# A hybrid encoder step on one core: norm weights beside x's rows, two weight loads on ScalarE's queue, and a newly recorded order

## The chip, the core and the metric

The kernel runs on one core of one Trainium2 chip. The metric is the device time of one execution in microseconds (us), as the median of several. The kernel before takes 340.26 us, the median of three runs (340.23 to 340.39).

## What is computed

One layer of a streaming encoder for 512 prompt tokens (with 256 memory tokens) and for 32 new tokens over caches of 512 to 1024 rows, all in float32:

```
z = rmsnorm(x, norm_mix_g) @ w_in            # 1024 -> 3880 columns: q, k, v and gate of A and B, q and gate of M, indexer
mk, mv = rmsnorm(mem, norm_mem_g) @ w_mem_kv
oa = attention over the own and the 8 earlier chunks, with a learned position bias   # 6 heads x 64
ob = attention over the keys that an indexer picks (top 128 of prompt, 256 of 1056)  # 6 heads x 64, rotary
om = attention over the 256 memory tokens                                            # 4 heads x 64
x  = x + concat(oa * silu(ga), ob * silu(gb), om * silu(gm)) @ w_out
y  = rmsnorm(x, norm_final_g)                # and the new k and v rows are outputs too
```

## The kernel before

**Split products.** Each large product is done as three matmuls in a rounded format: a factor v is rounded on ScalarE to `h` (`xTh`, `wh`, `oAh`), and `l = v - h` (`xTl`, `wl`, `oAl`) is made on VectorE or GpSimd; the product is `h*h + l*h + h*l`. x comes in turned: eight blocks of 128 columns of x, `xr`, each 128 partitions by 544 tokens (512 prompt, 32 sample). The norm weight of a row of `xr` is a scalar of its partition, so that `A.activation(..., scale=gT[0][:, k:k+1])` scales and rounds in one pass. `gT[0]` (`g_mix` in the trace) is a tile of its own, loaded by a small DMA.

**The order is recorded, not scheduled by a tool.** The helper class `Timed` (all instructions stand under line 411) hands each instruction to the engine's program at once and also to `Line`, a small planner inside the kernel that keeps a clock for each engine. Tasks are Python generators that yield the time at which they want to go on; `Line.run` issues TensorE's projections one after the other and lets waiting tasks slip in between. So numbers such as `HOLD`, `LAG` and `SURE`, the costs in `Line.cost` and `Line.rate`, and the lists `START` (first loads), `EARLY` and `LATE` (order of the projections) decide the order in which instructions stand on every engine, and nothing else.

**TensorE.** Most of its work uses the array as 128x128. Attention scores (`k,q`) use it as two tiles of 64 rows, attention outputs (`z,va`, `z,vb`) as two of 64 columns, and the products of the 32 sample tokens (`raw,xF`, `xr,gw`, `raw,oS`) as four of 32 columns. `divided` issues such a job: it waits up to `HOLD` us (in the planner's clock) for another such job and then issues them together. `places` counts the score tiles that may be live (`SCORES`).

**The start.** `x_load` loads x block by block, and for each block 296 columns of the indexer's weights (`raw`); `ahead_load` adds 128 columns of the first key projection `ka0`. All go out on SyncE's queue (SP). `index_group` multiplies the two as they come; before data is there, TensorE multiplies a tile of ones.

**Who makes `wl`.** `w_split` gives a subtraction to VectorE when GpSimd is 0.5 us behind VectorE in the planner's clock, else to GpSimd. The rotary embedding (`rope_t`) shuffles and multiplies on VectorE (`rq`, `kb`, `qb`); the last addition goes to the less loaded of the two. `picks` is the top-128 search (`ysel`, `m`) on VectorE; `sample_choice` finds the threshold for the 32 sample tokens.

Of the kernel before, what the change touches and what calls it, by code (L numbers as in the profile page):

```python
# [36 lines left out]
START = "xxxwwwwtrrrrrwmmrr"  # L37
SURE = 1.0
SLACK = 1.06
HOLD = 2.0  # L40
LAG = 0.3
# [52 lines left out]
class Line:  # L94
# [4 lines left out]
    def __init__(self):  # L99
        self.clk = {"PE": 1.35, "DVE": 0.7, "ACT": 0.9, "POOL": 1.2, "SP": 0.7}  # L100
# [60 lines left out]
    @staticmethod  # L161
    def lag(of, to):

        if of is None and to == "PE":
            return 0.3
        if of == to or of is None:
            return 0.127 if to == "DVE" else 0.09 if to == "POOL" else 0.0
        return 0.95 if of == "SP" else 0.26 if to == "PE" else 0.2 if of == "PE" else 0.06 if of == "POOL" else 0.15
# [69 lines left out]
    def rate(self):  # L238

        t = self.clk["SP"]  # L240
        return 340e3 if t < 1 else 170e3 if t < 2.3 else 330e3 if t < 7 else 310e3 if 11 < t < 22 else 370e3

    def op(self, eng, op, outs, ins, kw):
# [16 lines left out]
        d = (outs[0].size() * 4 / self.rate() if eng == "SP" else  # L260
# [33 lines left out]
    def begin(self, o, t):  # L294
        last = self.last
        o.start = t
        if o.eng == "SP":
            o.end = max(t + 1.3, last["DMA"]) + o.d
            o.after = {"SP": t + 0.45, "DMA": o.end}
# [12 lines left out]
        self.clk[o.eng] = o.end if o.eng != "SP" else t  # L312
# [127 lines left out]
def hybrid_step(ctx: ExitStack, tc: tile.TileContext, a: dict):  # L440
# [3 lines left out]
    V, G, A, PE, DMA = (Timed(line, n, e) for n, e in (("DVE", nc.vector), ("POOL", nc.gpsimd), ("ACT", nc.scalar),  # L444
                                                       ("PE", nc.tensor), ("SP", nc.sync)))
# [44 lines left out]
    def divided(k, issue):  # L490
# [3 lines left out]
        job = [k, issue, None, False]  # L494
        waiting.append(job)
        end = line.now() + HOLD
        while not job[3]:
            if len(waiting) == 1 and line.now() < end:
# [5 lines left out]
            for j in [job] + [j for j in waiting if j is not job]:  # L504
                if there(j[0]):
# [136 lines left out]

    def w_split():
        for i in range(len(w_list)):
# [26 lines left out]
            if i < 4:  # L671
                for kk in range(2):
                    yield line.at(raw[:, kk, :])
                    rounded(wh[:, kk, :], raw[:, kk, :])
                    yield line.at(wh[:, kk, :]) - 0.2
# [7 lines left out]
            tsub(V if i in WV or 0.5 < line.clk["POOL"] - line.clk["DVE"] else G, wl, raw, f(wh))  # L683
# [124 lines left out]
    gT = [cp.tile([P, NK], F32, name=n) for n in ("g_mix", "g_mem")]  # L808
# [1480 lines left out]
```

## Time and profile before

| | |
|---|---|
| median of the timed runs | 340.26 us |
| the profiled execution: own time / span in the trace | 340.1 us / 338.3 us |
| TensorE (PE) busy | 329.9 us, 98%, 2785 matmul records |
| VectorE (DVE), ScalarE (ACT), GpSimd (POOL) busy | 283.2, 219.9, 166.1 us |
| granted TensorE clock | 9 of ten or more in every fortieth of the span |
| HBM read / written | 39.95 / 6.16 MB |

The span is what the trace covers; the profiled execution's own time is 1.8 us longer. A matmul's duration in the trace overlaps its successor's, so what a matmul costs is read from start to start. PEld is the weight load that runs ahead of each matmul.

### The profile page before, as it was taken

Reading aid. Unit: us, or ns where it says so; the run is one execution under the profiler, and the core shown is the slowest. Engines: PE = TensorE matmul, PEld = TensorE weight load, DVE = VectorE, ACT = ScalarE, POOL = GpSimd, SP = SyncE. Lnnn points to the kernel's source line nnn. Section 1 sums busy time; section 2 is a strip of 40 time slices with the busy share of each in tenths; the row PEclk is TensorE's granted clock in tenths of the full one; section 3 lists DMA queues with packets and bytes.
Section 4 is the critical chain, followed back from the end, with each engine's and each line's share of the span. In section 5 each row is a group of like instructions: output and inputs, shape, how many; then the busy total and the mean of one; then the engine's idle time right before and its main releaser. Section 6 shows DMA issues by size and latency. Waiting matters only on the chain.

```text
span 338.3 us, 7679 instructions
## 1 busy us (share of the span) xinstructions
PE 329.9 (98%) x2785; PEld 296.4 (88%) x2785; DVE 283.2 (84%) x726; ACT 219.9 (65%) x523; POOL 166.1 (49%) x191
## 2 busy tenths in 40 slices
PE   8999999999999999999999999999999999999992
PEld 8979997999998989998999999899998776878682
DVE  3957878698989999699999999999979899865762
ACT  5838787898758786776776755532469446864362
POOL 2326261585453389246257764685338513361542
PEclk9999999999999999999999999999999999999999
DMA  7999763176539412314113343141332977002033
GB/s 219 382 302 344 202 219 105 33 216 160 157 84 304 143 58 58 94 37 136 49 33 74 103 140 97 48 117 42 98 127 65 334 296 273 0 2 95 0 114 152
DMA packets 44725, 46.61 MB, mean 138 GB/s; under 512 B 4400, under 2 KB 36720, under 8 KB 44688
## 3 DMA queue, kind: packets, MB, share of 16 engines
q1 hardware_dynamic: 44688, 46.13, 44.0%
q8 instruction: 22, 0.36, 0.4%
q14 instruction: 15, 0.12, 0.1%
HBM read 39.95 MB, written 6.16 MB: 136 GB/s over the span
## 4 chain that ended last, share of the span: by engine, by line
PE 80%; DVE 9%; issue 4%; POOL 3%; ACT 2%; DMA 1%; POOLq 0%; DVEq 0%; ACTq 0%
PE bank L411 80%; DVE gate L411 1%; DVE ysel L411 1%; DVE m L411 1%; DVE xr L411 1%; DMA raw<-in_w_mem_kv_dram 1%; DVE z L411 1%; DVE KSs L411 1%; POOL wl L411 1%; DVE rot L411 1%; POOL wI L411 1%; POOL rot L411 1%; DVE bi L411 0%; ACT junk L411 0%; POOL rs L411 0%
## 5 line engine op out<-in xcount | busy, mean ns | idle before, releaser
L411 POOL TENSOR_TENSOR wl<-raw,wh 128x512 fp32r<-128x512 f32 (+1 forms) x65 | 90.7, 1398 | 107.3 <-ACT wh L411 105.5
L411 PE MATMUL bank<-xTh,wh 128*128 128x272 f32 x352 | 77.0, 299 | 0.1
L411 ACT ACTIVATE wh<-raw 128x512 fp32r<-128x512 f32 (+3 forms) x85 | 52.0, 619 | 37.2 <-PE bank L411 11.8
L411 PE MATMUL bank<-xTh,wl 128*128 128x272 f32 x352 | 73.0, 288 | 0.0
L411 PE MATMUL bank<-xTl,wh 128*128 128x272 f32 x352 | 72.8, 288 | 0.0
L411 PEld LDWEIGHTS bank<-xTh,wh 128*128 128x128 f32 x352 | 55.6, 189 | 5.2 <-issue 4.1
L411 ACT ACTIVATE z<-z,st 128x128 f32<-128x128 f32 (+3 forms) x78 | 41.0, 549 | 22.9 <-DVE st L411 22.9
L411 PEld LDWEIGHTS bank<-xTh,wl 128*128 128x128 f32 x352 | 55.2, 189 | 0.6 <-issue 0.6
L411 PEld LDWEIGHTS bank<-xTl,wh 128*128 128x128 f32 x352 | 55.2, 188 | 0.5 <-issue 0.5
L411 PE MATMUL bank<-wh,xTh 128*128 128x384 f32 (+1 forms) x88 | 26.9, 336 | 0.0
L411 DVE MAX8 m<-ysel 128x8 f32<-128x256 f32 (+2 forms) x48 | 26.4, 550 | 0.1
L411 PE MATMUL bank<-wh,xTl 128*128 128x384 f32 (+1 forms) x88 | 26.2, 327 | 0.0
L411 PE MATMUL bank<-wl,xTh 128*128 128x384 f32 (+1 forms) x88 | 26.1, 326 | 0.0
L411 DVE MATCH_REPLACE8 ysel<-m,ysel 128x256 f32<-128x256 f32 (+2 forms) x48 | 26.0, 542 | 0.0
L411 DVE SCALAR_TENSOR_TENSOR ysel<-r,wI,ysel 128x256 f32<-128x256 f32 (+2 forms) x21 | 18.6, 885 | 4.2 <-ACT r L411 3.6
L411 ACT ACTIVATE junkS<-ysS,bi 128x1056 int8<-128x1056 f32 x16 | 18.7, 1168 | 4.2 <-DVE bi L411 4.1
L411 PE MATMUL bank<-ident,z 128*128 128x128 f32 (+1 forms) x162 | 21.2, 272 | 0.0
L411 PEld LDWEIGHTS bank<-ident,z 128*128 128x128 f32 (+1 forms) x162 | 17.8, 141 | 2.0 <-issue 0.7
L411 ACT COPY z<-bank 128x512 f32<-128x512 f32 (+2 forms) x31 | 15.2, 517 | 5.5 <-PE bank L411 3.9
L411 ACT ACTIVATE r<-bank 128x512 f32<-128x512 f32 (+3 forms) x30 | 14.0, 485 | 5.8 <-PE bank L411 5.0
L411 PEld LDWEIGHTS bank<-wh,xTh 128*128 128x128 f32 x88 | 15.8, 191 | 0.4 <-issue 0.4
L411 PEld LDWEIGHTS bank<-wl,xTh 128*128 128x128 f32 x88 | 15.7, 188 | 0.0
(286 smaller groups left out, 765.1 us busy)
## 6 DMA issues: line engine op xcount, KB each, us to landing
raw<-in_w_in_dram SPq DMA_DIRECT2D x42, 256.0 KB, 2.9
raw<-in_w_out_dram SPq DMA_DIRECT2D x16, 256.0 KB, 4.1
raw<-in_w_in_dram SPq DMA_DIRECT2D x8, 384.0 KB, 4.0
xr<-in_x_t_dram SPq DMA_DIRECT2D x8, 272.0 KB, 4.3
nat<-in_x_prompt_dram SPq DMA_DIRECT2D x4, 512.0 KB, 5.4
raw<-in_w_mem_kv_dram SPq DMA_DIRECT2D x8, 256.0 KB, 3.1
xr<-in_x_prompt_dram SPq DMA_DIRECT2D x4, 512.0 KB, 6.3
out_dram<-xr SPq DMA_DIRECT2D x4, 512.0 KB, 2.6
```

The source lines that it names most:

```text
L411: return fn(*args, **kw)
```

## The change

`x_t`, the turned x in HBM, gets the norm weights as a 545th column, so that each block of x brings its own; the DMA of `g_mix` goes. The first two weight loads (`DMA2`) are issued on ScalarE's queue. The first block's second half is rounded after the first weights, and the first two blocks are rounded in halves. The planner learns the second queue and other rates, `HOLD`, `LAG` and `SCORES` change, `EARLY` and `LATE` are reordered, `divided` takes a condition, and some subtractions, multiplications and additions are given to GpSimd outright.

```diff
-START = "xxxwwwwtrrrrrwmmrr"
+START = "xxxtwwwwrrrrrwmmrr"
...
-HOLD = 2.0
-LAG = 0.3
+LINK = False
+HOLD = 3.0
+LAG = 0.5
...
-EARLY = ("va", "ka1", "ka2", "mk", "mv", "qa0", "qa1", "ga0", "qa2", "ga1", "ga2", "qm0", "gm0", "qm1", "gm1")
+EARLY = ("va", "qa0", "ka1", "mk", "qa1", "mv", "ga0", "ka2", "qa2", "ga1", "ga2", "qm0", "gm0", "qm1", "gm1")
 AHEAD = "ka0"
-LATE = ("gb0", "kb0", "kb1", "qb0", "qb1", "kb2", "qb2", "vb", "gb1", "gb2")
+LATE = ("gb0", "kb1", "qb0", "kb0", "gb1", "qb1", "vb", "qb2", "gb2", "kb2")
...
-        return 340e3 if t < 1 else 170e3 if t < 2.3 else 330e3 if t < 7 else 310e3 if 11 < t < 22 else 370e3
+        return 340e3 if t < 1 else 250e3 if t < 2.3 else 345e3 if t < 7 else 310e3 if 11 < t < 22 else 370e3
...
-        return When(lambda: max(self.had(x) for x in tiles), SURE + (0.0 if self.now() < 40 else 0.0))
+        return When(lambda: max(self.had(x) for x in tiles), SURE + (0.5 if self.now() < 40 else 0.0))
...
-    def divided(k, issue):
+    def divided(k, issue, may=lambda: True):
...
-            if len(waiting) == 1 and line.now() < end:
+            if not may():
+                yield line.soon()
+                continue
+            if sum(j[4]() for j in waiting) == 1 and line.now() < end and not (LINK and any(j[0] and not j[4]() for j in waiting)):
...
-            tsub(V if i in WV or 0.5 < line.clk["POOL"] - line.clk["DVE"] else G, wl, raw, f(wh))
+            tsub(V if i in WV or 5.0 < line.clk["POOL"] - line.clk["DVE"] else G, wl, raw, f(wh))
...
-        DMA.dma_start(raw, w_in[k0 * P:k1 * P, c0:c0 + P].rearrange("(k p) n -> p k n", p=P))
+        (DMA if ahead else DMA2).dma_start(raw, w_in[k0 * P:k1 * P, c0:c0 + P].rearrange("(k p) n -> p k n", p=P))
...
-            tsub(V if c else V, wl, raw, f(wh))
+            tsub(G if c else V, wl, raw, f(wh))
...
-                DMA.dma_start(gT[0], a["norm_mix_g"])
-            DMA.dma_start(raw[:, kk, :], w_in[rows, QI:QI + 296])
+            (DMA if c + kk else DMA2).dma_start(raw[:, kk, :], w_in[rows, QI:QI + 296])
...
-                if k < 1:
+                if k < 2:
                     for j in range(2):
                         sl = slice(j * N // 2, (j + 1) * N // 2)
-                        yield line.at(t[:, kk, :])
-                        A.activation(h[:, sl], t[:, kk, sl], AF.Copy, scale=gT[0][:, k:k + 1])
+                        if k == 0 and j:
+                            yield from line.wait(lambda: w_k[0] or wh_0)
+                        yield line.at(x)
+                        A.activation(h[:, sl], x[:, sl], AF.Copy, scale=g)
...
-            V.tensor_tensor(t, t, ctab["sin64"][:, sl], op=ALU.mult)
+            G.tensor_tensor(t, t, ctab["sin64"][:, sl], op=ALU.mult)
             yield line.at(t, out) - 0.2
-            least(out, V, G).tensor_tensor(out, t, out, op=ALU.add)
+            G.tensor_tensor(out, t, out, op=ALU.add)
...
-        yield from line.wait(lambda: count["scored"] >= len(TILES) and "kb2" in over)
+        yield from line.wait(lambda: count["scored"] >= len(TILES) and "picks" in over)
...
-    SCORES = 9
+    SCORES = 8
...
-        pair = Pair(0, hp, lambda hp=hp: both(split_q(queried[0][:, hp, 0:S], 1.0, G), split_of(natural["ka"][:, hp, 0:S], 1.0, V, "k")), lambda: va)
+        pair = Pair(0, hp, lambda hp=hp: both(split_q(queried[0][:, hp, 0:S], 1.0, G), split_of(natural["ka"][:, hp, 0:S], 1.0, G, "k")), lambda: va)
...
-    arrays["x_t"] = np.ascontiguousarray(np.concatenate([arrays["x_prompt"], arrays["x_sample"]]).T)
+    g = np.asarray(inputs["norm_mix_g"]).reshape(1, D)
+    arrays["x_t"] = np.ascontiguousarray(np.concatenate([arrays["x_prompt"], arrays["x_sample"], g]).T)
```

What this does to the order of instructions, at three places. First the start of ScalarE's program, before; `xTh` is the rounded x, `wh` a rounded weight (296 columns of the indexer's, 128 or 384 of `ka0`'s):

```order
L411 ACT_TABLE_LOAD
L411 ACTIVATE m_73<-nhalf 128x1
L411 ACTIVATE xTh_79<-xr,g_mix 128x272 x2
L411 ACTIVATE wh<-raw 128x296
L411 ACTIVATE wh<-raw 128x128
L411 ACTIVATE wh<-raw 128x296
L411 ACTIVATE xTh_79<-xr,g_mix 128x544
L411 ACTIVATE wh<-raw 128x384
```

And with the change:

```order
L412 DMA raw<-in_w_in_dram 128x296
L412 DMA raw<-in_w_in_dram 128x128
L412 ACT_TABLE_LOAD
L412 ACTIVATE m_73<-nhalf 128x1
L412 ACTIVATE xTh_79<-xr 128x272
L412 ACTIVATE wh<-raw 128x296
L412 ACTIVATE xTh_79<-xr 128x272
L412 ACTIVATE wh<-raw 128x128
L412 ACTIVATE wh<-raw 128x296
L412 ACTIVATE xTh_79<-xr 128x272 x2
L412 ACTIVATE wh<-raw 128x384
```

Two loads now stand ahead of ScalarE's first instruction, `g_mix` is gone, and the first weight's rounding lies between the halves of the first block of x. On SyncE's queue the second block of x is now the third DMA; it was the sixth.

Second, TensorE at the end of the indexer's group, before. `raw,xF` (the sample tokens' products) and `xr,gw` (the indexer's first keys) use the array as four tiles of 32 columns:

```order
L411 MATMUL bank<-raw,xF 32x296 x8
L411 MATMUL bank<-xTl_82,wh 128x272 x2
L411 MATMUL bank<-wh,xTh_81 128x296 x3
L411 MATMUL bank<-wl,xTh_81 128x296 x3
L411 MATMUL bank<-wh,xTl_82 128x296 x3
L411 MATMUL bank<-xTh_81,wh 128x272 x2
L411 MATMUL bank<-xTh_81,wl 128x272
L411 MATMUL bank<-raw,xF 32x384 x8
L411 MATMUL bank<-xTh_81,wl 128x272
L411 MATMUL bank<-xTl_82,wh 128x272 x2
L411 MATMUL bank<-xr,gw 32x128 x8
```

And with the change:

```order
L412 MATMUL bank<-wh,xTl_82 128x296 x3
L412 MATMUL bank<-xTh_81,wh 128x272 x2
L412 MATMUL bank<-xTh_81,wl 128x272 x2
L412 MATMUL bank<-xTl_82,wh 128x272 x2
L412 MATMUL bank<-xr,gw 32x128 x8
L412 MATMUL bank<-raw,xF 32x296 x8
L412 MATMUL bank<-raw,xF 32x384 x8
L412 MATMUL bank<-wh,xTh_79 128x384
```

Three departures from the 128x128 array have become one. Over the whole program TensorE's matmuls are the same but for two of the ten with ones; the array changes its tile shape 78 times where it did 88 times, and it leaves 128x128 33 times where it did 39 times (counted over the order of both built programs).

Third, GpSimd in the last third of the program, before (`rq`, `kb`, `qb` belong to the rotary embedding of B's keys and queries):

```order
L411 TENSOR_TENSOR kb<-rq,kb 128x272 x2
L411 TENSOR_TENSOR wl<-raw,wh 128x512 x2
L411 TENSOR_TENSOR qb<-rq,qb 128x272 x2
L411 TENSOR_TENSOR wl<-raw,wh 128x512 x2
L411 TENSOR_TENSOR qb<-rq,qb 128x272 x2
L411 TENSOR_TENSOR wl<-raw,wh 128x768
```

And with the change, around B's last queries:

```order
L412 TENSOR_TENSOR wl<-raw,wh 128x512 x4
L412 TENSOR_TENSOR rq<-rq,sin_124 128x272 x2
L412 TENSOR_TENSOR wl<-raw,wh 128x512
L412 TENSOR_TENSOR qb<-rq,qb 128x272 x2
L412 TENSOR_TENSOR wl<-raw,wh 128x512 x4
```

The multiplications `rq<-rq,sin` (twelve in the program) have come over from VectorE, in front of the additions. With them came three `kl<-ka,k`, nine `wl` and three `gate` products (each two instructions on GpSimd).

## Rows read from the trace of the kernel before

**Rows 1.** The page's part 1: busy time, share of the span and instructions of engines.

```profile
PE 329.9 (98%) x2785; PEld 296.4 (88%) x2785; DVE 283.2 (84%) x726; ACT 219.9 (65%) x523; POOL 166.1 (49%) x191
```

**Rows 2.** Busy time of each engine in stretches of the span: stretch, then us busy (and instructions) of PE, PEld, DVE, ACT, POOL, then granted clock, DMA share and GB/s.

```profile
10.00:20.00 10.00, 10.00 (x81) 9.65 (x83) 7.83 (x14) 7.32 (x13) 4.16 (x6) 1.00 1.08 361
...
120.00:130.00 10.00, 10.00 (x102) 8.70 (x100) 9.82 (x34) 7.76 (x21) 9.88 (x10) 1.00 0.22 52
...
190.00:220.00 30.00, 30.00 (x274) 28.31 (x273) 29.64 (x73) 18.50 (x51) 17.52 (x17) 1.00 0.35 101
```

**Rows 3.** TensorE's instructions in order of time at the start: start, us, what, partitions and elements, count.

```profile
5.36 0.91 PE L411 MATMUL bank<-wh,xTh 128*128 128x296 f32 x3
...
6.52 0.57 PE L411 MATMUL bank<-wh,xTl 128*128 128x296 f32 x3
...
7.68 0.62 PE L411 MATMUL bank<-wh,xTh 128*128 128x296 f32 x3
```

**Rows 4.** SyncE's queue in order of time: when a DMA is issued and how long the issue takes.

```profile
0.73 0.38 SPq L411 DMA_DIRECT2D xr<-in_x_t_dram  x1
1.16 0.42 SPq L411 DMA_DIRECT2D g_mix<-in_norm_mix_g_dram  x1
1.63 1.37 SPq L411 DMA_DIRECT2D raw<-in_w_in_dram  x3
3.04 0.43 SPq L411 DMA_DIRECT2D xr<-in_x_t_dram  x1
```

**Rows 5.** DMA issues between 0.7 and 5 us: size of one, and median us from issue to landing.

```profile
raw<-in_w_in_dram SPq DMA_DIRECT2D x3, 148.0 KB, 3.2
...
g_mix<-in_norm_mix_g_dram SPq DMA_DIRECT2D x1, 4.0 KB, 2.5
```

**Rows 6.** The loads of x's blocks (tile `xr`) in the first 14 us, from issue to landing.

```profile
DMA to landing us min/median/max: 2.8/4.3/4.7
```

**Rows 7.** ScalarE in order of time at the start; in brackets the idle time before it and what ended it.

```profile
3.79 0.93 ACT L411 ACTIVATE xTh<-xr,g_mix 128x272 fp32r<-128x272 f32 x2 [1.57 <-DMA g_mix<-in_norm_mix_g_dram]
4.85 1.15 ACT L411 ACTIVATE wh<-raw 128x296 fp32r<-128x296 f32 x3
6.82 0.75 ACT L411 ACTIVATE xTh<-xr,g_mix 128x544 fp32r<-128x544 f32 x1 [0.81 <-DMA xr<-in_x_t_dram]
```

**Rows 8.** VectorE in order of time at the start: the remainder of the first block of x.

```profile
4.76 0.79 DVE L411 SCALAR_TENSOR_TENSOR xTl<-xr,g_mix,xTh 128x544 fp32r<-128x544 f32 x1 [3.77 <-ACT xTh L411]
```

**Rows 9.** TensorE in order of time around one attention score (`k,q`): the array's rows*columns stand before the partitions and elements.

```profile
105.62 0.41 PE L411 MATMUL bank<-xTl,wh 128*128 128x272 f32 x2
105.87 0.41 PE L411 MATMUL bank<-xTh,wl 128*128 128x272 f32 x2
106.21 0.50 PE L411 MATMUL bank<-k,q 64*128 64x512 f32 x2
106.55 0.40 PE L411 MATMUL bank<-k,ql 64*128 64x512 f32 x2
106.78 0.39 PE L411 MATMUL bank<-kl,q 64*128 64x512 f32 x2
107.10 0.52 PE L411 MATMUL bank<-xTh,wh 128*128 128x272 f32 x2
107.45 0.41 PE L411 MATMUL bank<-xTl,wh 128*128 128x272 f32 x2
```

**Rows 10.** TensorE in order of time around the first sample product.

```profile
19.18 0.41 PE L411 MATMUL bank<-xTh,wl 128*128 128x272 f32 x2
19.52 1.20 PE L411 MATMUL bank<-raw,xF 128*32 128x296 f32 x16
20.65 0.52 PE L411 MATMUL bank<-xTl,wh 128*128 128x272 f32 x2
21.01 0.57 PE L411 MATMUL bank<-wh,xTh 128*128 128x296 f32 x3
```

**Rows 11.** TensorE in order of time around one step of `sample_choice` (`bf_ok,over`).

```profile
154.85 0.41 PE L411 MATMUL bank<-xTh,wl 128*128 128x272 f32 x2
155.62 0.16 PE L411 MATMUL bank<-bf_ok,over 128*128 128x1 bf16 x1 [0.36 <-ACT bf_ok L411]
```

**Rows 12.** Groups of instructions on GpSimd and VectorE, by shape: count, then busy us, mean ns of one, and idle us before them.

```profile
L411 POOL TENSOR_TENSOR wl<-raw,wh 128x512 fp32r<-128x512 f32 x60 | 81.3, 1358 | 99.1 <-ACT wh L411 97.3 <-PE bank L411 0.9 <-DVE bi L411 0.4
L411 POOL TENSOR_TENSOR wl<-raw,wh 128x768 fp32r<-128x768 f32 x5 | 9.4, 1884 | 8.2 <-ACT wh L411 8.2
L411 POOL TENSOR_TENSOR tg<-tg,gate 128x272 f32<-128x272 f32 x9 | 8.0, 894 | 8.6 <-ACT tg L411 8.6
...
L411 DVE TENSOR_TENSOR rq<-rq,sin 128x272 f32<-128x272 f32 x12 | 11.2, 969 | 0.0
L411 DVE SCALAR_TENSOR_TENSOR gate<-tg,gate 128x272 f32<-128x272 f32 x7 | 5.7, 831 | 0.8 <-ACT tg L411 0.7
L411 DVE TENSOR_TENSOR wl<-raw,wh 128x512 fp32r<-128x512 f32 x5 | 4.2, 835 | 0.6 <-ACT wh L411 0.6
```

**Rows 13.** VectorE, and then GpSimd, in order of time from 217.8 us on.

```profile
218.06 3.36 DVE L411 TENSOR_TENSOR rq<-rq,sin 128x272 f32<-128x272 f32 x2
...
217.85 1.28 POOL L411 TENSOR_TENSOR oMl<-o,oMh 128x512 fp32r<-128x512 f32 x1
219.09 2.03 POOL L411 TENSOR_TENSOR wl<-raw,wh 128x768 fp32r<-128x768 f32 x1
```

More of the change, by code (lines that the diff above doesn't have):

```diff
@@ L259, in op @@
                     deps.setdefault(o, False)
-        d = (outs[0].size() * 4 / self.rate() if eng == "SP" else
+        d = (outs[0].size() * 4 / self.rate(eng) if eng in ("SP", "SQ") else
              self.cost(eng, op, outs, ins, kw) * (1.0 if eng == "PE" else SLACK))
@@ L296, in begin @@
         o.start = t
-        if o.eng == "SP":
+        if o.eng in ("SP", "SQ"):
             o.end = max(t + 1.3, last["DMA"]) + o.d
-            o.after = {"SP": t + 0.45, "DMA": o.end}
+            o.after = {o.eng: t + 0.45, "DMA": o.end}
         else:
@@ L311, in begin @@
         o.enter(last)
-        self.clk[o.eng] = o.end if o.eng != "SP" else t
+        self.clk[o.eng] = o.end if o.eng not in ("SP", "SQ") else t
     def events(self):
@@ L504, in divided @@
             for j in [job] + [j for j in waiting if j is not job]:
-                if there(j[0]):
+                if there(j[0]) and j[4]():
                     waiting.remove(j)
@@ L807, in hybrid_step @@
     mTl = []
-    gT = [cp.tile([P, NK], F32, name=n) for n in ("g_mix", "g_mem")]
+    g_mem = cp.tile([P, NK], F32, name="g_mem")
     x_raw, x_done, m_raw, m_done, rows_in = [], [0], [], [0], []
@@ L924, in m_split @@
             t = m_raw[k // 4][:, k % 4, :]
-            yield max(line.at(t, gT[1]), line.clk["ACT"])
-            yield from part(mTh[k // 4][:, k % 4, :], mTl[k // 4][:, k % 4, :], t, gT[1][:, k:k + 1])
+            yield max(line.at(t, g_mem), line.clk["ACT"])
+            yield from part(mTh[k // 4][:, k % 4, :], mTl[k // 4][:, k % 4, :], t, g_mem[:, k:k + 1])
             m_done[0] += k % 2
@@ L1010, in start @@
                 load_tables(32)
[L1011 removed]
+                DMA.dma_start(g_mem, a["norm_mem_g"])
         allowed[0] = len(w_list)
@@ L1990, in attend @@
         k = 2 * len(u.rows)
-        yield from line.wait(lambda: places[0] >= k)
-        places[0] -= k
         if pair.q is None:
@@ L1996, in attend, with begin @@
         yield line.sure(*pair.q, *pair.k)
-        sc = yield from divided(k, u.begin)
+        def begin():
+            places[0] -= k
+            return u.begin()
+        sc = yield from divided(k, begin, lambda: places[0] >= k)
         count["scored"] += 1
@@ L2008, in attend, with mix @@
         yield line.sure(*(z for r in u.z for z in r))
-        o = yield from divided(1, lambda: u.mix(bank()))
-        places[0] += k
+        def mix():
+            places[0] += k
+            return u.mix(bank())
+        o = yield from divided(1, mix)
         count["mixed"] += 1
```

36 lines of the change are left out of this document (19 added, 17 removed).

## The prediction

> **What bounds the kernel now.** I read the engines' busy time first, then the stretches, then TensorE in order of time. TensorE is busy for 329.9 of 338.3 us, VectorE for 283.2, GpSimd for 166.1 [rows 1]; in a stretch from the thick of the kernel TensorE is busy all the time while VectorE (9.82 of 10) and GpSimd (9.88 of 10) are too, and from 190 to 220 us VectorE is busy for 29.64 of 30 [rows 2]. So TensorE sets the time and the others only just keep up. Since the busy time of overlapping matmuls hides gaps, the starts have to be read. There the reader sees three kinds of loss. The first real matmul starts at 5.36 us [rows 3]. Each time the array changes its shape, the starts stand further apart than their work [rows 9, 10]. And now and then TensorE waits for a result, as for `bf_ok` at 155 us [rows 11]. The change touches all three. Its matmuls are otherwise those of before, so what is won or lost is won or lost in these gaps; behind the last matmul the same instructions follow as before, and I put nothing there.
>
> The sum is made against the profiled execution's own 340.1 us; the median of the runs is 0.16 higher, and I add that at the end. A change within 0.2% of 340.26, about 0.7 us, is what the measurement of this kernel cannot tell from none.
>
> **The start.** Before, ScalarE rounds the first block of x from 3.79 on, released by `g_mix` [rows 7], which was issued at 1.16 and takes 2.5 to land, 3.66 [rows 4, 5]. The block itself was issued at 0.73; the shortest landing of such a block is 2.8, so it is there at 3.53 [rows 4, 6]. Dropping `g_mix` alone is therefore worth about 0.1 us. The first weights are later than both: the first of three issued from 1.63 on, 3.2 to land, 4.83 [rows 4, 5], and ScalarE takes them at 4.85 [rows 7]. On ScalarE's queue they go out beside x, nearly 0.9 us sooner; what that costs ScalarE, two issues of some 0.4 us, lies in the time in which it waits for data anyway.
>
> When does x land then? At best at 3.53 as before. At worst it shares the DMA engines with both loads that now start beside it (148 and 64 KB): 212 KB at the 361 GB/s of the stretch from 10 to 20 us [rows 2] are 0.59 us, so 4.12. From there ScalarE needs a half of x (0.47, half of 0.93), the weights (about 0.4, a third of 1.15) and the other half (0.47) [rows 7], and VectorE 0.79 for `xTl` [rows 8]; with 0.1 of handing over that is 2.25, so `xTl` is there between 5.8 and 6.4. TensorE multiplies by it from 6.52 on before [rows 3]. The gain in the first eighth is 0.1 to 0.7. The second eighth must be there too: before, it starts at 7.68 [rows 3], just behind the rounding of the second block (6.82 + 0.75) [rows 7], which had been issued at 3.04 [rows 4]. In the new order that block is SyncE's third DMA, at about 1.6, and does not hold this gain up. I take 0.35 us, between the bounds of 0 (the sharing costs all) and 0.7. Behind it TensorE already goes at its pace, so the gain stays.
>
> The Trainium skill, "DMA: Bandwidth & Descriptors", section "Issuing engines are not separate DMA queues", speaks against more: DMAs of several engines run on the same DMA engines and interleave, so a second queue saves issue time alone. By that rule x lands at the late end and the start gives about 0.1; by the issue times in the rows it gives up to 0.7.
>
> **Fewer changes of the array's shape.** A pair of matmuls on the full array takes 0.25 us from start to start (105.62 to 105.87) [rows 9]. Into `k,q` it takes 0.34 (105.87 to 106.21), 0.09 more. Out of it, a `kl,q` pair takes 0.32 (106.78 to 107.10), where the pair before took 0.23: 0.09 more. And the first pair back on the full array takes 0.35 (107.10 to 107.45), 0.10 more. Leaving the full array and coming back thus costs 0.28 us. The sample product shows the same where it can be read: 0.34 into it (19.18 to 19.52) and 0.36 for the first pair after it (20.65 to 21.01) [rows 10], 0.20 without the way out. The new order leaves the full array 33 times instead of 39: 6 x 0.28 = 1.7 us less. Of the 88 changes 10 went from one small shape to another without coming back, of the 78 now 12 do: two more at about 0.09, 0.2 us. Net -1.5 us; as bounds -1.2 (only 0.20 each) and -1.9 (0.35 each, where the way out of a sample product costs as much as both others). That is nearest to a sure gain, since nothing else runs on TensorE meanwhile. The two matmuls with ones that are dropped lie in the wait at the start and are worth nothing; without that wait they would be worth two of them.
>
> **The old waits.** At 155 us a pair takes 0.77 (154.85 to 155.62) where 0.25 is the rule [rows 11], so 0.5 us are lost to `bf_ok`, which stood behind other work on ScalarE and VectorE. The new order puts other work there; I count half of it as gone, -0.25, with 0 and -0.5 as bounds.
>
> **Work from VectorE to GpSimd.** Twelve `rq` products (11.2 us on VectorE), five `wl` of 512 (4.2), four smaller `wl`, three `kl` and three gate products (0.83 each) leave VectorE, some 22 us of 283 [rows 12]. On GpSimd they are 12 x 0.89 (by `tg`, of the same size), 8 x 1.36, 1.88, three small `wl` at about 0.9 (estimated between) and 3 x 2 x 0.89: 31 us on top of 166 [rows 1, 12]. In total both have room, 261 and 197 of 338, and TensorE covers it; but one such subtraction takes 1.36 instead of 0.84, and what queues behind it on GpSimd is the next `wl`, for which TensorE's next projection waits. No row shows how often the cover fails in the new order. From below it is 0 (the moved work is as well hidden as GpSimd's is today, where its `wl` wait 97 us for ScalarE and not TensorE for them) [rows 12]; from above I take 3.5 us, a few whole GpSimd subtractions. I take 0.5, nearer to the lower end because of those 97 us.
>
> **Sum.** 340.1 - 0.35 - 1.5 - 0.25 + 0.5 = 338.5; with 0.16 for the runs 338.7 us, 0.5% faster.
>
> **Rivals.**
> GpSimd becomes the one that is waited for, and the kernel is slower. For it: between 120 and 130 us GpSimd is full already, and at 218 us two `rq` on VectorE take 3.36 us instead of about 1.9 while GpSimd makes `oMl` and a `wl` [rows 2, 12, 13]; each holds the other up, and GpSimd now has 31 us more. Against it: the same rows show that `rq` is what suffers, and that it leaves VectorE. The place is the projections between 100 and 250 us. It decides from about two subtractions that TensorE waits out in full (2 x 1.36 is more than the 2.1 gained); three such and one `wl` of 768 give 340.26 - 2.1 + 3 x 1.36 + 1.88 = 344, two and a short wait 341.5. I use 342.
> The Trainium skill, "SBUF — State Buffer", section "Who interferes with whom", has it that VectorE and GpSimd share a pair of ports that one instruction holds alone to its end; the two `rq` at 218 us agree. By that rule alone the longer GpSimd instructions cost VectorE more than the move saves, the same rival.
>
> B's last keys: `kb2` is now the last projection, its rotary part runs on GpSimd, and the last attention units come behind it. If their `z` are late, TensorE waits with only the output product to fill in; a wait of 1.5 us eats what the shapes give: 340.2, no change. Against it: the output products and `z,vb` of earlier units are left as filler.
>
> The start gives nothing, since x shares with the weights: 338.7 + 0.35 = 339.0, still faster.
>
> Relief of VectorE shows: no new waits, no `bf_ok` wait, the full start: 340.26 - 0.7 - 1.5 - 0.5 = 337.6.
>
> **Chances.** Forecast 0.52, start without gain 0.13, relief 0.08: faster by over 0.2% 0.73. Same, by `kb2` or a like wait, 0.14. Slower, by GpSimd, 0.13. The likeliest alone lies between 337.6 (all lower bounds but the relief's) and 339.5. For 8 in 10 the range goes from 337.3 (shapes at -1.9 with the relief) up through the cases without change to 341.0; above it lies most of the slower case.
>
> **What would show it.** In the changed trace: `xTh` no longer released by a small DMA and starting between 3.6 and 4.2; the second eighth on TensorE between 7.0 and 7.6; one departure from the full array near 20 us instead of three; pairs at 0.25 between; GpSimd's busy time near 197 and VectorE's near 261. The last matmul should end some 1.6 us sooner than before, and as long before the span's end. It would be wrong if TensorE shows waits for `wl` or `z` of more than 1 us in sum, if x lands later than 4.2, or if the granted clock falls because TensorE idles at the start with two matmuls with ones fewer.

## The result, and the profile after

The changed kernel takes 337.59 us (median of five, 337.37 to 338.2); the kernel before, beside it, 340.39 (340.23 to 340.57). The ratio is 0.992, 95% interval 0.9906 to 0.9935: 0.8% faster. The profiled execution took 337.59 us itself, against 340.1 before: 2.5 us to explain.

Engines' busy time, the page's part 1 of the changed kernel (before: [rows 1]):

```profile
PE 327.5 (98%) x2781; PEld 296.2 (88%) x2781; DVE 270.2 (80%) x698; ACT 218.3 (65%) x525; POOL 196.4 (58%) x221
```

Some 30 us more on GpSimd, as worked out, but only 13 fewer on VectorE, not 22: what stayed there takes longer in sum. Eight `wl` of 296 columns take 0.75 us each instead of 0.50 and seven `ysel` of 512 columns 1.08 instead of 0.82, while seven `ysel` of 384 columns became faster (0.90 instead of 1.08). TensorE is as full as it was.

**The start.** ScalarE in order of time (before: [rows 7]), then SyncE's queue, then TensorE (before: [rows 3]):

```profile
0.72 0.89 ACTq L412 DMA_DIRECT2D raw<-in_w_in_dram  x2
...
3.93 0.52 ACT L412 ACTIVATE xTh<-xr 128x272 fp32r<-128x272 f32 x1 [0.79 <-DMA xr<-in_x_t_dram]
4.35 0.43 ACT L412 ACTIVATE wh<-raw 128x296 fp32r<-128x296 f32 x1
```

```profile
1.63 0.42 SPq L412 DMA_DIRECT2D xr<-in_x_t_dram  x1
```

```profile
4.84 0.95 PE L412 MATMUL bank<-wh,xTh 128*128 128x296 f32 x3
...
7.34 0.57 PE L412 MATMUL bank<-wh,xTh 128*128 128x296 f32 x3
```

x itself now ends ScalarE's wait, at 3.93, later than the 3.53 it would reach alone; the second block goes out at 1.63 instead of 3.04; and the second eighth (the products of x's second block) starts at 7.34 where it started at 7.68. The first matmul gains more, 0.52 us, but the first eighth takes 2.50 us where it took 2.32.

**The array's shapes.** TensorE at the end of the indexer's group (before: [rows 10]). One way out of the full array, and both kinds of small products behind each other:

```profile
20.94 0.41 PE L412 MATMUL bank<-xTl,wh 128*128 128x272 f32 x2
21.28 0.65 PE L412 MATMUL bank<-xr,gw 128*32 128x128 f32 x16
21.74 2.47 PE L412 MATMUL bank<-raw,xF 128*32 128x296 f32 x32
```

**The waits.** What TensorE waited for (engine and result waited for, us in total, times, longest), before and then after, each without the wait for the ones at the very start:

```profile
PE bank L411 <- DVE KSs L411: 0.5, 1, 0.5
PE bank L411 <- ACT bf_ok L411: 0.4, 1, 0.4
```

```profile
PE bank L412 <- ACT ysS L412: 0.9, 1, 0.9
```

Two old waits are gone and one new one has come. The list leaves out short ones: by the starts a matmul is 0.21 us late at 181 us before, and one waits 0.26 us for `k` at 28.7 us after. The first of the old ones, for `KSs` (the sample's indexer keys), my prediction did not have. Its rows in the kernel before, VectorE, GpSimd and TensorE in order of time:

```profile
49.01 2.35 DVE L411 TENSOR_TENSOR KSs<-cbi,KSs 64x1024 fp32r<-64x1024 f32 x1
```

```profile
48.98 1.29 POOL L411 TENSOR_TENSOR wl<-raw,wh 128x512 fp32r<-128x512 f32 x1 [0.55 <-ACT wh L411]
```

```profile
50.76 0.28 PE L411 MATMUL bank<-KS,QS 128*128 128x256 f32 x1
51.50 0.70 PE L411 MATMUL bank<-KSs,QSs 128*128 128x512 f32 x2 [0.46 <-DVE KSs L411]
```

After the change the same subtraction, and what GpSimd does beside it:

```profile
46.42 1.22 DVE L412 TENSOR_TENSOR KSs<-cbi,KSs 64x1024 fp32r<-64x1024 f32 x1
```

```profile
46.47 1.59 POOL L412 TENSOR_TENSOR rs<-ss,nhalf 128x1 f32<-128x1 f32 x1 [2.40 <-DVE ss L412]
```

Here VectorE starts first and takes 1.22 us; the small GpSimd instruction that starts 0.05 us behind it takes 1.59, where five of the six others like it take 0.55. Before, the subtraction started 0.03 us behind a `wl` of 1.29 and took 2.35, nearly the sum of the two, and TensorE's start-to-start of 0.74 where 0.12 is usual is 0.6 us lost. The Trainium skill, "SBUF — State Buffer", section "Who interferes with whom", says that a VectorE instruction with two inputs in SBUF contends with a GpSimd instruction that reads SBUF, and that the ports they share are held exclusively; these rows agree.

In the new wait VectorE is held up in the same way. The changed kernel around 58 us, GpSimd, VectorE, ScalarE and TensorE:

```profile
57.76 1.28 POOL L412 TENSOR_TENSOR wl<-raw,wh 128x512 fp32r<-128x512 f32 x1 [4.00 <-ACT wh L412]
```

```profile
56.80 0.48 DVE L412 SCALAR_TENSOR_TENSOR ysel<-r,wI,ysel 128x256 f32<-128x256 f32 x1 [2.37 <-ACT r L412]
57.99 1.33 DVE L412 SCALAR_TENSOR_TENSOR ysel<-r,wI,ysel 128x256 f32<-128x256 f32 x1 [0.70 <-ACT r L412]
...
59.74 0.43 DVE L412 COPY ysS<-bank 64x256 f32<-64x256 f32 x1
```

```profile
60.20 0.37 ACT L412 COPY ysS<-bank 64x256 f32<-64x256 f32 x1 [1.39 <-DVE ysS L412]
```

```profile
59.27 0.46 PE L412 MATMUL bank<-identR,stk 128*128 128x128 f32 x4
60.62 0.54 PE L412 MATMUL bank<-identR,stk 128*128 128x128 f32 x4 [0.89 <-ACT ysS L412]
```

The reader should see the chain from above: the second `ysel` takes 1.33 us instead of 0.48 beside the `wl`; the `ysS` copy queued behind it (after one more product, 0.47) comes at 59.74; ScalarE's copy waits for that one; and TensorE, which needs the bank, stands for about 1.0 us. A `ysel` held up by a `wl` is not new: before, one took 1.32 us at 59.47, beside a `wl` at 59.24, and TensorE did not wait. New is what stands behind it.

### The profile page after: what moved, and what is told of

It reads as the page before. It is cut to its first block, busy times and chain, and to the rows that moved or that the text cites. A ratio compares the mean times of both kernels' runs of the same rounds, so it can differ in the third digit from the quotient of the medians.

```text
span 335.8 us, 7696 instructions
## 1 busy us (share of the span) xinstructions
PE 327.5 (98%) x2781; PEld 296.2 (88%) x2781; DVE 270.2 (80%) x698; ACT 218.3 (65%) x525; POOL 196.4 (58%) x221
## 4 chain that ended last, share of the span: by engine, by line
PE 96%; issue 1%; ACT 1%; DVE 1%; POOLq 0%; POOL 0%; ACTq 0%
PE bank L412 96%; DVE xr L412 0%; ACT r L412 0%; ACT sq L412 0%; POOLq L2284 0%; ACT wh L412 0%; DVE mTl L412 0%; DVE ysS L412 0%; ACT mTh L412 0%; ACT ysS L412 0%; POOL xr L412 0%; POOL ss L412 0%; DVE ones L412 0%; DVE ysel L412 0%; ACTq L412 0%
## 5 line engine op out<-in xcount | busy, mean ns | idle before, releaser
L412 POOL TENSOR_TENSOR wl<-raw,wh 128x512 fp32r<-128x512 f32 (+3 forms) x74 | 102.2, 1388 | 81.7 <-ACT wh L412 65.6
L412 ACT ACTIVATE z<-z,st 128x256 f32<-128x256 f32 (+3 forms) x77 | 40.4, 548 | 17.9 <-DVE st L412 17.8
L412 DVE SCALAR_TENSOR_TENSOR ysel<-r,wI,ysel 128x256 f32<-128x256 f32 (+2 forms) x21 | 19.7, 940 | 6.1 <-ACT r L412 5.1
L412 PE MATMUL bank<-ident,z 128*128 128x128 f32 (+1 forms) x162 | 20.1, 271 | 0.0
L412 DVE TENSOR_TENSOR xr<-bank,xr 128x512 f32<-128x512 f32 (+1 forms) x17 | 11.2, 657 | 8.4 <-PE bank L412 5.8
L412 ACT COPY z<-bank 128x512 f32<-128x512 f32 (+1 forms) x31 | 15.1, 538 | 4.0 <-PE bank L412 3.8
```

What stands on the lines that cost most here:

```text
L412: return fn(*args, **kw)
```

## The experiments

My theory was the prediction's sum: departures from the full array give most, the start 0.35, waits and the move to GpSimd little. The rivals were that the start or the queue gives nothing, that shape changes are hidden and waits explain the gain, and that relief of VectorE is what counts.

**What a departure costs (e2, e3).** In the changed kernel, at the end of each of 21 projections, past the planner, one of these; e3 has the second line:

```diff
+        PE.engine.matmul(acc[1][:, 384:512], wl[0:64, 0, :], xTh[1][0:64, 0, 0:P], start=True, stop=True, tile_position=(0, 0))
...
+        PE.engine.matmul(acc[1][:, 384:512], wl[:, 0, :], xTh[1][:, 0, 0:P], start=True, stop=True)
```

> The changed kernel with one extra matmul of 128 columns on a tile of 64 rows at the end of each of 21 projections; what it writes is read by nobody, and the planner does not know of it. The array leaves 128x128 51 times instead of 33, 18 more, and changes its shape 115 times instead of 78. To be compared with the next kernel, which has the same 21 matmuls on the full array. Theory (leaving and coming back costs 0.28 us each): 18 x 0.28 = 5.0 us more than that one, with 3.6 (0.20 each) and 6.3 (0.35 each) as bounds. Rival (a change of shape costs nothing that isn't hidden, and the gain came from waits that went): within 0.5 us of that one.

> The same 21 extra matmuls on the full 128x128 array; 33 departures as in the change. Both theories: 21 matmuls of 128 columns at 0.053 us (128 columns at 2.4 GHz) to 0.12 us each, so 1.1 to 2.5 us above the change's 337.59.

Measured: e2 345.41 us (345.28 to 345.86), e3 339.55 (the median of twelve; its profiled execution took 341.26, so its trace is not used for the price). The difference of 5.86 us over 18 departures is 0.33 each; e3 alone puts an extra full matmul at (339.55 - 337.59) / 21 = 0.09. One such place in e2, TensorE in order of time:

```profile
92.51 0.41 PE L412 MATMUL bank<-xTh,wl 128*128 128x272 f32 x2
92.86 0.32 PE L797 MATMUL bank<-xTh,wl 64*128 64x128 f32 x1
93.11 0.52 PE L412 MATMUL bank<-xTh,wh 128*128 128x272 f32 x2
93.46 0.41 PE L412 MATMUL bank<-xTl,wh 128*128 128x272 f32 x2
```

The pair before it takes 0.35 instead of 0.25, the extra matmul 0.25 instead of 0.09, the first pair after it 0.35 instead of 0.25: 0.36 in sum. The theory holds, the price being a little higher than the 0.28 read off the trace; the rival of hidden shape changes falls.

**The second queue (e1).** Edit, in the changed kernel:

```diff
-                                                       ("PE", nc.tensor), ("SP", nc.sync), ("SQ", nc.scalar)))
+                                                       ("PE", nc.tensor), ("SP", nc.sync), ("SQ", nc.sync)))
```

> The changed kernel with its first two weight loads issued on SyncE's queue again, in the same place of the program; the recorded order of every other engine is that of the change. Theory (the queue gives the start its 0.35 us): the first weights go out about 0.45 us later, behind x, and x's second block two issues (0.9 us) later, so TensorE's second eighth starts 0.2 to 0.7 us later than 7.34 us and the kernel takes 337.8 to 338.3 us. Rival (loads share the same DMA engines, so a second queue saves nothing): x lands a little earlier, the weights little later, and the time stays within 0.1 us of the change's 337.59.

Measured: 338.18 us (338.03 to 338.25), 0.6 more than the change. ScalarE and TensorE at the start of it:

```profile
3.55 0.52 ACT L412 ACTIVATE xTh<-xr 128x272 fp32r<-128x272 f32 x1 [1.33 <-DMA xr<-in_x_t_dram]
...
6.49 0.94 ACT L412 ACTIVATE xTh<-xr 128x272 fp32r<-128x272 f32 x2 [0.31 <-DMA xr<-in_x_t_dram]
```

```profile
4.48 1.25 PE L412 MATMUL bank<-wh,xTh 128*128 128x296 f32 x3
5.54 0.94 PE L412 MATMUL bank<-wl,xTh 128*128 128x296 f32 x3
...
7.60 0.58 PE L412 MATMUL bank<-wh,xTh 128*128 128x296 f32 x3
...
8.84 0.41 PE L412 MATMUL bank<-xTh,wh 128*128 128x272 f32 x2
9.18 0.52 PE L412 MATMUL bank<-xTh,wl 128*128 128x272 f32 x2
9.53 0.41 PE L412 MATMUL bank<-xTl,wh 128*128 128x272 f32 x2
```

GpSimd in it:

```profile
7.92 1.20 POOL L412 TENSOR_TENSOR wl<-raw,wh 128x384 fp32r<-128x384 f32 x1 [0.74 <-ACT wh L412]
```

With the weights' loads behind it x lands 0.38 us sooner, and the first matmul starts 0.36 sooner than in the change. The second block's rounding waits for its load until 6.49 (5.65 in the change) and ends at 7.43, and the second eighth comes 0.26 later. But TensorE does not wait for that block: from 6.85 on its pairs stand 0.25 apart, and the second eighth follows the first without a gap. The first eighth itself takes 3.12 us instead of 2.50, at the slower pace of the last section. What the late block costs comes after that. ScalarE's next weights stand behind its rounding, the `wl` that GpSimd makes of them ends at 9.12 instead of 8.37 (7.06 + 1.31 in the change), and TensorE, which needs it, takes up the next pair 0.34 us behind the one before, and the one after that 0.35, instead of 0.25. The lag grows from 0.27 to 0.46 there, and 0.49 it is at the last matmul.

So in this trace about 0.2 us is what the queue gains by sending the second block out sooner; the other 0.26 us is the slower pace, which need not come from the edit. The rival, within 0.1 us, is out by the time of the whole kernel, 0.6 more in the median of five. The Trainium skill, "DMA: Bandwidth & Descriptors", section "Issuing engines are not separate DMA queues", lets a second queue save issue time alone. The trace agrees: with the loads beside it x landed later, and the 0.2 us come from an issue that went out sooner (1.63 instead of 2.57). The 0.1 us that the prediction took from that rule for the whole start was too little.

**The new wait taken away (e4).** One `ysS` copy goes to ScalarE, the planner still booking it on VectorE:

```diff
-                        either(ysS[64 * c:64 * c + 64, k0 + j * m:k0 + (j + 1) * m], p[64 * j:64 * j + 64, 0:m])
+                        either(ysS[64 * c:64 * c + 64, k0 + j * m:k0 + (j + 1) * m], p[64 * j:64 * j + 64, 0:m], AV)
```

> The changed kernel with one copy of the sample scores (ysS, 64x256) on ScalarE instead of VectorE; every other instruction stands where it stood. Theory (TensorE's wait of 1.03 us at 59.5 us comes from VectorE, whose product ysel took 1.33 us beside a GpSimd subtraction and held up that copy): the copy is done near 59.2 instead of 60.2, TensorE's wait shrinks by 0.5 to 1.0 us, and the time is 336.6 to 337.1 us. Rival (the wait has another cause, or the gap opens again at the next wait behind it): 337.4 to 337.8 us.

Measured: 336.57 us (336.39 to 336.91), ratio to before 0.989 (0.9878 to 0.9903): the whole wait, and faster than both kernels. ScalarE and TensorE:

```profile
58.71 0.37 ACT L536 COPY ysS<-bank 64x256 f32<-64x256 f32 x1
59.09 0.37 ACT L412 COPY ysS<-bank 64x256 f32<-64x256 f32 x1
```

```profile
59.16 0.89 PE L412 MATMUL bank<-identR,stk 128*128 128x128 f32 x8
```

`ysel` is as slow as in the change (1.33 us at 57.88); only nothing that TensorE needs stands behind it any more.

**Where the work stands (e9, e6, e11, e10).** Four kernels ask what the move from VectorE to GpSimd does. In e9, e6 and e11 the planner keeps its old belief, so TensorE's order is exactly that of the kernel they start from. `VG` is GpSimd booked as VectorE, `GV` VectorE booked as GpSimd. In e9, from before (with the `kl`, the late `wl` and those of the start likewise, nine `wl` in all; the three gate products stay):

```diff
-            V.tensor_tensor(t, t, ctab["sin64"][:, sl], op=ALU.mult)
+            VG.tensor_tensor(t, t, ctab["sin64"][:, sl], op=ALU.mult)
```

> The kernel before with the same kinds of work moved to GpSimd (twelve rq products, three kl, the late wl and those of the start), the planner believing them on VectorE, so that TensorE's order and its 39 departures are exactly those of before. Theory A (relief of VectorE pays in any order): 339.5 us or less. Theory B (a place on an engine pays only in the order that was recorded with it, and the work put back in the changed kernel cost 4 us because the order was recorded for GpSimd): 340.2 to 344 us, with new waits on TensorE for z, wl or a result of VectorE.

Measured: 340.14 us, ratio 0.9999 (0.999 to 1.0008), with VectorE's busy time down to 271.9 and GpSimd's up to 186.9. TensorE's waits in it are the two of before, 0.5 us for `KSs` and 0.4 for `bf_ok`.

In the order of before the move is worth nothing: no wait goes and none comes. Theory A is out, and the new waits of theory B did not come either. The other way round, in e6 from the change:

```diff
-            G.tensor_tensor(t, t, ctab["sin64"][:, sl], op=ALU.mult)
+            GV.tensor_tensor(t, t, ctab["sin64"][:, sl], op=ALU.mult)
...
-            tsub(V if i in WV or 5.0 < line.clk["POOL"] - line.clk["DVE"] else G, wl, raw, f(wh))
+            tsub(V if i in WV else GV if 0.5 < line.clk["POOL"] - line.clk["DVE"] else G, wl, raw, f(wh))
```

> The changed kernel with the subtractions (nine wl by the old rule, three kl, those of the start) and the twelve rq products back on VectorE in the same places; the planner believes them on GpSimd, so that TensorE's order and array shapes are exactly those of the change. Theory (the move to GpSimd is not what made the kernel faster, it only costs or saves single waits): 337.2 to 338.6 us. Rival 1 (relief of VectorE made the gain): 339 us or more. Rival 2 (the longer GpSimd instructions hold VectorE up and cost TensorE more than one wait): below 337.0.

Measured: 341.67 us (340.87 to 344.5), 4.1 more than the change: the theory missed, and the time is the one that rival 1 gave. But the edit puts back more than had been moved. The planner books the work on GpSimd, so the old rule finds GpSimd behind oftener: 17 `wl` came back to VectorE, where the change had moved nine, and VectorE is busy for 285.2 us, more than before. So 4.1 us is not the price of the move, and rival 1 is not shown. The profiled execution was the longest of its runs, so its waits are not added up here; but in it the `ysS` wait stands at 0.9 us as in the change, with the `wl` beside its `ysel` on GpSimd even by the old rule. That wait is therefore not a child of the move.

> The changed kernel with the twelve rq products alone back on VectorE, TensorE's order unchanged. They stand behind 150 us, so the waits of the kernel with all work put back that lie before 130 us (start, k at 29, bf_ok at 105) must be gone, and of its 4 us those for z and for VectorE behind 150 us remain if rq is their cause: 338.3 to 340 us. If rq is not their cause, 337.4 to 337.9.

e11, the first hunk of e6 alone: 338.73 us (its profiled execution 338.75), 1.1 more than the change. VectorE and TensorE in it, and then VectorE in the change:

```profile
201.68 0.78 DVE L412 TENSOR_TENSOR rq<-rq,sin 128x272 f32<-128x272 f32 x2
...
203.77 1.28 DVE L412 TENSOR_REDUCE st<-bank 128x2 f32<-128x512 f32 x2
```

```profile
206.16 1.09 PE L412 MATMUL bank<-z,mv 128*64 128x128 f32 x16 [0.70 <-ACT z L412]
```

```profile
201.34 1.29 DVE L412 TENSOR_REDUCE st<-bank 128x2 f32<-128x512 f32 x2 [0.63 <-PE bank L412]
```

The `rq` on VectorE, these two and those before them, push the reduction for `st` from 201.34 to 203.77; `z` is late by as much as TensorE cannot cover, and it waits. So the twelve rq alone are worth about 1 us in the order of the change; what the `kl` and the nine `wl` are worth in it was not measured.

e10 takes the moves back by the old rules and lets the planner know it, so that the order is recorded anew. Of the `wl` 13 go to VectorE by the rule, not nine.

```diff
-            G.tensor_tensor(t, t, ctab["sin64"][:, sl], op=ALU.mult)
+            V.tensor_tensor(t, t, ctab["sin64"][:, sl], op=ALU.mult)
...
-            tsub(G if c else V, wl, raw, f(wh))
+            tsub(V if c else V, wl, raw, f(wh))
```

> The changed kernel with the moves to GpSimd taken back and the planner knowing it, so that the order is recorded anew for this placement: 38 departures and 85 changes of shape instead of 33 and 78. Theory B: five departures more are 1.4 to 1.65 us, and the waits are of the size that a new record brings, 0 to 3 us: 339 to 342 us, below the 341.67 of the kernel with the same placement in the order recorded for the other. Theory A (VectorE's load itself makes the waits): 342 us or more.

Measured: 343.29 us (343.2 to 343.75), above the range I gave theory B and in that of theory A. Five more departures are 1.6 us; what I had not allowed for is one wait of 2.0 us and what followed it. It is for `bf_ok`, and this is the stretch behind it (columns as in [rows 2]):

```profile
171.00:175.00 4.00, 3.85 (x20) 3.75 (x20) 3.78 (x12) 3.97 (x11) 1.77 (x2) 0.57 0.00 0
```

The granted clock is at 0.57 for 4 us, nearly all of it at the lower level of 1.2 GHz; 4 x 0.43 = 1.7 us more of full pace are lost. Since VectorE's load and the new record changed together, theory A is not told from theory B here. Together the four kernels say: placement and order are not two gains that add. In the order of before nearly all of the move changed the time by 0.1 us; in that of the change the twelve rq alone are worth 1.1, and with 17 `wl` and the `kl` 4.1; and a new record for the old rules, with the change's other numbers, was worse still. Whether another choice of numbers would give VectorE's placement a good order stays open.

**Holding jobs together (e7).**

```diff
-HOLD = 3.0
+HOLD = 0.0
```

> The changed kernel with HOLD at 0 instead of 3, so that a job on tiles no longer waits for another one: the array leaves 128x128 36 times instead of 33 and changes shape 84 times instead of 78. The recorded order changes with it, so waits may come and go. Theory (0.28 to 0.33 us for each departure with its return): 0.85 to 1.0 more for the three departures, 338.4 to 338.6 us if waits are as in the change; what differs from that must be seen as single waits in the trace. Rival (departures are not what the time follows): within 0.3 us of 337.59 without waits that make up for it.

Measured: 342.7 us (342.26 to 342.8), 5.1 more. Three departures at 0.33 are 1.0 of it. Most of the rest are waits that a new record brought, the largest in total:

```profile
PE bank L412 <- DVE z L412: 1.1, 2, 0.9
```

With 0.7 for `cacheM` and 0.6 for `k` these are 2.4 us in sum, and the change's wait for `ysS` is not among e7's. Added up from the starts, all waits together are 2.5 us more than in the change. The matmuls beside a change of shape take 1.5 to 2.2 us more beyond their usual interval, by how many neighbours are counted, so the departures cost more here than 1.0. The expected 338.4 to 338.6 supposed the waits of the change, which this record does not have.

**The lists (e8).**

```diff
-EARLY = ("va", "qa0", "ka1", "mk", "qa1", "mv", "ga0", "ka2", "qa2", "ga1", "ga2", "qm0", "gm0", "qm1", "gm1")
+EARLY = ("va", "ka1", "ka2", "mk", "mv", "qa0", "qa1", "ga0", "qa2", "ga1", "ga2", "qm0", "gm0", "qm1", "gm1")
...
-LATE = ("gb0", "kb1", "qb0", "kb0", "gb1", "qb1", "vb", "qb2", "gb2", "kb2")
+LATE = ("gb0", "kb0", "kb1", "qb0", "qb1", "kb2", "qb2", "vb", "gb1", "gb2")
```

> The changed kernel with the lists EARLY and LATE of before: 34 departures and 80 changes of shape. Theory: one departure more, 0.3 us, so 337.9 us plus or minus single waits of up to 1 us that the new order of projections makes or removes. Rival (the order of the projections is what removed the old waits): a wait of 0.5 us or more at the steps of the sample search or at KSs comes back and the time is 338.5 us or more.

Measured: 345.55 us (344.22 to 347.13; the profiled execution 347.13), 8 more than the change for one departure more. The rival on record for e8 holds: a wait for `bf_ok` is back, with 0.9 us. And the prediction's rival with a chance of 0.13, a GpSimd that is waited for, is here too. GpSimd and TensorE in order of time:

```profile
125.08 1.26 POOL L412 TENSOR_TENSOR kl<-ka,k 128x512 fp32r<-128x512 f32 x1
126.31 1.45 POOL L412 TENSOR_TENSOR wl<-raw,wh 128x512 fp32r<-128x512 f32 x1
```

```profile
127.81 0.82 PE L412 MATMUL bank<-xTh,wl 128*128 128x272 f32 x2 [2.70 <-POOL wl L412]
```

A `kl` that came over from VectorE stands in front of the next projection's `wl`, and TensorE waits out two GpSimd subtractions, in the stretch from 100 to 250 us that the prediction named. That is 2.7 us of the 9.5 by which the profiled execution is longer; its other waits (for `tg` 1.0, `bf_ok`, `wh`, `z` and `zS`) make 3.2, and the lower clock behind the long one (the last section) 7 x 0.40 = 2.8.

**The start alone (e5).** The change's `x_t`, `x_load`, `x_split` and `DMA2` in the kernel before, everything else as it was:

```diff
-        DMA.dma_start(raw, w_in[k0 * P:k1 * P, c0:c0 + P].rearrange("(k p) n -> p k n", p=P))
+        (DMA if ahead else DMA2).dma_start(raw, w_in[k0 * P:k1 * P, c0:c0 + P].rearrange("(k p) n -> p k n", p=P))
...
-            DMA.dma_start(raw[:, kk, :], w_in[rows, QI:QI + 296])
+            (DMA if c + kk else DMA2).dma_start(raw[:, kk, :], w_in[rows, QI:QI + 296])
```

> The kernel before with the part of the change that concerns the start alone: norm weights in x's column, no g_mix load, the first two weight loads on ScalarE's queue, the first two blocks rounded in halves. Planner's numbers, lists and VectorE's work are those of before; the array leaves 128x128 39 times as before. Theory (the start is worth 0.35 us, the rest comes from fewer departures and from waits): 339.7 to 340.1 us, with the waits at 50.8 and 155 us still there. Rival (the start gives nothing, x shares with the weights): 340.2 to 340.5. Other rival (the start carries most of the gain): 338.5 or less.

Measured: 342.27 us (341.94 to 342.36), 2 us slower than before (ratio 1.0058, 1.0046 to 1.007). Against before, the same matmul stands 0.32 us earlier at 31 us and still 0.17 earlier at 268 us: the start's gain is there. Then the record, shifted by the new start, asks for B's cached keys some 7 us sooner than before, while their loads go out at 264 us and 269.6, hardly sooner than before (264 and 270.5). TensorE:

```profile
274.80 0.80 PE L411 MATMUL bank<-keysB,qbS 64*32 64x352 f32 x8 [0.44 <-DMA keysB<-in_cache_b_k_dram]
276.75 1.97 PE L411 MATMUL bank<-keysB,qbS 64*32 64x352 f32 x28 [1.16 <-DMA keysB<-in_cache_b_k_dram]
```

That is 1.6 us of idle time, about 2.2 by the starts, given back at the other end of the kernel. The time lies outside all three ranges on record, since none allowed for a wait that the new record itself makes.

**A second fix (e12).** e4, and the first weights' load behind x on SyncE's queue (`DMA3`), the load of `ka0` staying on ScalarE's:

```diff
-            (DMA if c + kk else DMA2).dma_start(raw[:, kk, :], w_in[rows, QI:QI + 296])
+            (DMA if c + kk else DMA3).dma_start(raw[:, kk, :], w_in[rows, QI:QI + 296])
```

> The kernel with the ysS copy on ScalarE (336.57 us), and the first 296 columns of weights on SyncE's queue behind x; only the 128 columns of ka0 stay on ScalarE's. Theory: x shares with 64 KB less at first and lands up to 0.3 us earlier, the second block of x goes out one issue (0.45 us) later, which its rounding (5.65 us) does not notice: 336.2 to 336.5 us. Rival (the second block or its weights are what counts, as when both loads stood on SyncE's queue): 336.7 to 337.1 us.

Measured: 336.96 us (336.81 to 337.15), 0.4 slower than e4, with ranges that overlap by 0.1. (The load that moves is the one of 148 KB, not of 64.) x did land sooner by 0.1, and the second block 0.2 later, but neither decides in the trace: the first matmul starts within 0.04 us of e4's and the second eighth comes 0.67 later, because TensorE takes the first eighth at a slower pace (the last section). My expectation missed it; the rival's time came, but its cause is not shown.

## Why the prediction was right, and where it was wrong

338.7 us was forecast and 337.59 measured: faster, inside the range, 1.1 us off. By its steps:

| step | forecast | measured |
|---|---|---|
| start | -0.35 | -0.34 at the second eighth (7.68 to 7.34), in one execution of each |
| shape changes | -1.5 | -1.8 (6 x 0.33 less 2 x 0.09, by the price of e2) |
| old waits | -0.25 | -1.3 (`KSs` 0.6, `bf_ok` 0.5, a smaller one at 181 us 0.2) |
| new waits | +0.5 | +1.3 (`ysS` 1.0, `k` at 28.7 us 0.3) |
| behind the last matmul | 0 | -0.2, cause open |
| sum | -1.6 | -2.3, of 2.5 in the profiles |

**The start** had the right size, its bounds and the late landing of x as well; e5 agrees (7.43). The size holds at the usual pace: of the ten traces with both loads on ScalarE's queue nine have the second eighth between 7.23 and 7.54, but e2 has it at 8.01. The reason was half right: I had the first weights' earlier issue as the gain and the second block as no hindrance. In e1 the late second block costs 0.2 us.

**The shapes** are the largest term and the safest one. e2 against e3 confirms the reading of three row pairs, 0.33 instead of 0.28. Added up from the starts in the two traces, the matmuls beside a change of shape take 1.5 to 2.3 us less beyond their usual interval than before, by how many neighbours are counted; the 1.8 lies between.

**The old waits** were mis-sized by a factor of five. I listed `bf_ok` and halved it, and passed over `KSs`, which stands above it in the list of TensorE's waits. Both were in the trace of before, and both are gone.

**The new waits** are the step that failed as reasoning. I put +0.5 on the move from VectorE to GpSimd. In the order of before that move costs nothing (e9). The 1.0 us that appeared is a GpSimd subtraction that holds VectorE up, the mechanism of the slower rival, but not one of the moved ones (e6 keeps the wait). And in the new order the twelve rq would cost 1.1 us if they had stayed on VectorE (e11), which the forecast had nowhere. That the net came out near the sum is partly luck: the two wait terms were wrong by -1.05 and +0.8 and nearly cancel.

**Sums and signs.** Three figures of the prediction are slightly off, with no effect on the forecast: the steps from x to `xTl` add up to 2.23, not 2.25; the smaller bound of the shapes leaves out the 0.2 of the two extra changes and should be -1.0; and the relief with the shapes at -1.9 gives 337.2, not 337.3. Of the signs that were named, the start of `xTh` (3.93), the second eighth (7.34), the one departure near 20 us and GpSimd's 196.4 us came. VectorE's time did not (270.2, not 261), and the last matmul ends 2.3 us sooner, not 1.6.

**The rivals.** GpSimd waited for: not in the changed kernel, yet with the lists of before (e8) it is, for 2.7 us. `kb2` late: no such wait appeared. The start without gain: 7.34 and e5's 7.43 against 7.68 speak against it, though the pace of a single execution (the last section) can move that point by more. Relief: the time is the one it gave, 337.6, but not by its terms, since the start gave half and a new wait came. The chance of 0.13 for a slower kernel may well have been too low in another sense: e5, e7, e8 and e10, all records made with some of these numbers changed, were 2 to 5 us slower than before. The departures of the change's order could be counted ahead; its waits could not be told from its parts.

## What to carry to other kernels

Where a planner writes one long order, price the order as a whole: count its departures from the full array, at a price read from start to start, and read the list of what the bounding engine waits for to the end, because that list is what a new order rewrites. Do not add up parts: each of the four orders recorded here with only a part of the change was 5 to 8 us slower than the change, in waits above all. Where the order can be held fixed, hold it and change one thing; e4 and e11 could be traced to one wait each, the new records could not. And look for a small result that the bounding engine needs and that is queued on VectorE behind an instruction with two SBUF inputs while GpSimd works; moving that one copy gave 1.0 us, over a third of what the whole change gave.

## What the runs showed of the hardware

A wait of TensorE can cost more than itself. Behind the wait of 2.0 us in e10 the granted clock was at 0.57 for the 4 us from 171 to 175, then 1.00 again to 180; behind the one of 2.7 us in e8 it was 0.60 over the next 7 us. Behind the 1.0 us of the changed kernel and a wait of 1.6 us in e3 it stayed at 1.00. The stretch of e8:

```profile
128.00:135.00 7.00, 7.00 (x54) 6.07 (x55) 5.39 (x22) 1.60 (x5) 6.92 (x8) 0.60 0.51 128
```

And the first matmuls have a pace of their own. In e12 the second group of three, 296 columns each, takes 0.74 us from start to start, 0.25 for one, what 296 columns take at 1.2 GHz; in the change it is 0.44, and 0.42 later on:

```profile
4.70 1.27 PE L412 MATMUL bank<-wh,xTh 128*128 128x296 f32 x3
5.77 0.94 PE L412 MATMUL bank<-wl,xTh 128*128 128x296 f32 x3
6.51 0.80 PE L412 MATMUL bank<-wh,xTl 128*128 128x296 f32 x3
```

The matmuls with ones ahead of them are the same in both, the data was there, and the granted clock of those stretches reads 1.00 in either profile, so the slower pace is seen in the starts alone. e1 shows it too, and so does e2, whose start is the change's own, instruction by instruction:

```profile
4.90 1.27 PE L412 MATMUL bank<-wh,xTh 128*128 128x296 f32 x3
...
8.01 0.58 PE L412 MATMUL bank<-wh,xTh 128*128 128x296 f32 x3
```

The other nine traces with both loads on ScalarE's queue take 2.49 or 2.50 us for the first eighth; e2 takes 3.11, e1 3.12 and e12 3.20. So the pace can differ between executions of the same start. Whether the edits of e1 and e12 bring the slow one about, and what decides it, was not found. It moves the second eighth by 0.6 to 0.7 us, as much as the whole time of e1 differs from the change and more than that of e12 from e4.
